# Attention probabilities copied by a DMA into a float32r tile ahead of their transposes, with one raw weight buffer less and one 4 KB buffer more

## The chip, the core and the metric

The kernel runs on one core of a Trainium2 chip. Its time is the device time of one execution in microseconds (us). Three runs of the kernel before took 1148.66 to 1150.13 us, with a median of 1149.91 us. The core has five engines that run beside one another, each through its own list of instructions in a fixed order: TensorE (PE; its weight loads are listed as PEld), VectorE (DVE), ScalarE (ACT), GpSimd (POOL) and SyncE (SP). A DMA is issued by an instruction on one of these lists and then runs on 16 DMA engines that all lists share.

## The reference

Two blocks of one kind, and then a third of another kind, work on 256 tokens of width 1024 in float32. The change touches only the attention of the first two blocks:

```python
sc = jnp.einsum('bqkgd,bskd->bkgqs', qi, ki) * scale          # banded, masked
m = jnp.maximum(jnp.max(sc, axis=-1, keepdims=True), sink_f)
p = jnp.exp(sc - m)
denom = jnp.sum(p, axis=-1, keepdims=True) + jnp.exp(sink_f - m)
o = jnp.einsum('bkgqs,bskd->bqkgd', p / denom, vi)
```

There are 16 query heads of 64 columns on 4 key/value heads, so four query heads share one key/value head. Around the attention, a block projects its normed input to queries, keys, values, three convolution inputs and two gates, mixes attention and convolution through the gates and an output matrix, and then runs a gated feed-forward part of width 2816. The third block has another attention, a pooling part, the same feed-forward shape, and gates made from a conditioning vector.

## The kernel before

**Weights.** All weights lie in DRAM in the order of their use, as 211 pieces of 1 MB. `emit_raw` (L253) loads a piece in two halves of 512 KB on SP's queue into tiles with the tag `raw`, of which there are `NRAW` = 7. `emit_half` (L266) splits each half into a high part `H` (a cast to float32r on ACT, L278) and a low part `L` (a subtraction on DVE, L280); 12 halves of each can stand ready (`NSPLIT`). A raw buffer comes free when its subtraction is done. `get` (L284) is called where a piece is used; it emits the loads and the splits some pieces ahead. Pieces of the conditioning matrix are not split; DVE reduces them straight from the raw tile (L524).

**Matmuls.** The projections are sums of three products of such parts (`mmB` L439, `mmA4` L460, `mmD2` L477). All matmuls made through the helper `mm` bear the line L247.

**Attention.** In each of the first two blocks `attention` (L595) starts eight generators `unit(g, t)`, one for each key/value head g (0 to 3) and each half t of the tokens. A unit goes through these steps:

- L634 and L635: the queries of four heads are split into a high and a low part; L640: four transposes of float32r tiles against `ident_r`; L643: a copy out of PSUM.
- L650 and L651: eight matmuls give the scores S of four heads; L654 to L662: mask, row maximum and bias on DVE.
- L666: four exponentials on ACT write the tile P (128 x 4 x 256, float32, 4 KB in each partition) and its row sums; L668 to L671: denominators; L673: four ACT instructions scale P by the reciprocals.
- L681: eight transposes of 128 x 128 float32 blocks of P against the float32 identity `ident`, in two PSUM tiles of four (the first pair of heads, then the second); L683: ACT copies each PSUM tile into PT.
- For t = 1 the unit goes on to the products of PT with the values (L692).

So there are 16 units and 128 transposes at L681 in all. P and PT are tiles with the tag `s4` (4 KB in each partition, `NS4` = 17 buffers), which also holds activations and gain rows.

**What sets the order.** The kernel's own clock counts time in matmuls: `pe(ns)` (L222) is called behind each group of matmuls with a planned duration, and `tick()` (L225), which is called at a few points inside each projection, resumes the generators that are due. A generator says by `yield d` that it wants to go on d us of this clock later. Between L673 and L681 stands `yield SM_DELAY`, 8.0. The units start `UNIT` = 10 us of this clock apart, beside the convolution projections (`pcc`, `pcx`, `pcb`, `pcp` in the trace). The framework's planner then makes each engine's list from this order, by priorities and its own reckoning of how long each instruction takes: an instruction whose inputs it reckons not to be there yet is passed by others that are. At run time each list is worked through in its order, and an instruction whose input is late holds up all that stand behind it on its engine.

Of the kernel before, what the change touches and what calls it, by code (L numbers as in the profile page):

```python
# [10 lines left out]
F32 = mybir.dt.float32  # L11
F32R = mybir.dt.float32r
# [6 lines left out]
P = 128  # L19
D = 1024  # L20
T = 256
# [12 lines left out]

WARM = 13
WARM2 = 4
NRAW = 7
NSPLIT = 12
LOOK = 3
LOOK_RAW = 5  # L40
NS4 = 17
NS2 = 7
PRIO = 30
TR_DELAY = (6.0, 7.5)
# [2 lines left out]
MIX_DELAY = 2.5  # L47
WO2_LEAD = 2
UNIT = 10.0
SM_DELAY = 8.0  # L50
SOFT = 30
ST_DELAY = 8.0
ST_STEP = 3.5
# [109 lines left out]
def tile_model(ctx: ExitStack, tc: tile.TileContext, x_in, wpack, sink, convw, gains, c_in,  # L163
               b_cond, w_pool, pool_scale, ident_c, rope_c, amask_c, smask_c, tri_c, pmat_c, out):
    nc = tc.nc
# [7 lines left out]
    def s4(name, shape=(P, D), dt=F32):  # L173
        return ac.tile(list(shape), dt, tag="s4", name=name, bufs=NS4)

    def s2(name, shape=(P, 512), dt=F32):
        return ac.tile(list(shape), dt, tag="s2", name=name, bufs=NS2)

    def ps1(name, shape=(P, 512), dt=F32):
        return pp.tile(list(shape), dt, tag="B", name=name, bufs=8)  # L180

    def small(name, n, dt=F32):
        return sm.tile([P, n], dt, tag="sm", name=name, bufs=24)
# [35 lines left out]
    def spawn(gen, delay=0.0):  # L219
        tasks.append([clock[0] + delay, gen])  # L220

    def pe(ns):  # L222
        clock[0] += ns / 1000.0
# [22 lines left out]
    def mm(o, a, b, start, stop, **kw):  # L246
        nc.tensor.matmul(o, a, b, start=start, stop=stop, **kw)  # L247
# [5 lines left out]
    def emit_raw():  # L253
        i, hf = divmod(state["raw"], 2)
        t = wp.tile([P, CH // 2], F32, tag="raw", name=f"raw{i}_{hf}", bufs=NRAW)
        if state["raw"] == 1:
# [55 lines left out]
    ident = cst.tile([P, P], F32, tag="ident", name="ident")  # L312
# [20 lines left out]
    ident_r = cst.tile([P, P], F32R, tag="identr", name="ident_r")  # L333
# [261 lines left out]
    def attention(l, q, kf, v, op):  # L595
        kTh = s4(f"kTh{l}", (P, NKV, T), F32R)
        kTl = s4(f"kTl{l}", (P, NKV, T), F32R)

        def rotate(src, n, t, tg):
            q3 = src.rearrange("p (h d) -> p h d", d=HD)  # L600
            ra = s2(f"r{tg}{l}{t}", (P, 2, n, 16))
            ct = rope[:, t, 0:16].unsqueeze(1).to_broadcast([P, n, 16])
            s0 = rope[:, t, 16:24].unsqueeze(1).to_broadcast([P, n, 8])
            s1 = rope[:, t, 24:32].unsqueeze(1).to_broadcast([P, n, 8])
            nc.vector.tensor_mul(ra[:, 0], q3[:, :, 0:16], ct)
            nc.vector.tensor_mul(ra[:, 1, :, 0:8], q3[:, :, 8:16], s0)
            nc.vector.tensor_mul(ra[:, 1, :, 8:16], q3[:, :, 0:8], s1)
            nc.vector.tensor_add(q3[:, :, 0:16], ra[:, 0], ra[:, 1])

        def keys(t):  # L610
            rotate(kf[t], NKV, t, "k")
            kd = [s2(f"kd{j}{l}{t}", (P, NKV, 2, HD), F32R) for j in range(2)]
            k3 = kf[t].rearrange("p (g d) -> p g d", d=HD)
            for u in range(2):
                nc.scalar.copy(kd[0][:, :, u, :], k3)
            for u in range(2):
                nc.vector.tensor_sub(kd[1][:, :, u, :], k3, kd[0][:, :, u, :].bitcast(F32))
            yield 3.0
            for j, dst in enumerate((kTh, kTl)):
                pk = ps1(f"pk{j}{l}{t}", (P, 4, P), F32R)  # L620
                kdf = kd[j].rearrange("p g u d -> p (g u d)")
                for g in range(NKV):
                    nc.tensor.transpose(pk[:, g, :], kdf[:, g * P:(g + 1) * P], ident_r)
                    pe(64)
                nc.scalar.copy(dst[:, :, t * P:(t + 1) * P], pk.bitcast(F32))
            rotate(q[t], NH, t, "q")
            yield None

        PT = {}

        def unit(g, t):
            qs = s2(f"qs{l}{g}{t}", (P, 4, 2, HD), F32R)
            q3 = q[t].rearrange("p (h d) -> p h d", d=HD)[:, 4 * g:4 * g + 4, :]
            nc.scalar.copy(qs[:, :, 0, :], q3)  # L634
            nc.vector.tensor_sub(qs[:, :, 1, :], q3, qs[:, :, 0, :].bitcast(F32))  # L635
            yield 2.5
            pq = ps1(f"pq{l}{g}{t}", (P, 4, P), F32R)
            qf = qs.rearrange("p h u d -> p (h u d)")
            for hh in range(4):
                nc.tensor.transpose(pq[:, hh, :], qf[:, hh * P:(hh + 1) * P], ident_r)  # L640
                pe(64)
            qT = s2(f"qT{l}{g}{t}", (P, 4, P), F32R)
            nc.scalar.copy(qT, pq.bitcast(F32))  # L643
            yield 2.5
            S = [ps1(f"S{l}{g}{t}{i}", (P, 2, T)) for i in range(2)]
            hs = slice(P, 2 * P) if t == 0 else slice(0, P)
            m = small(f"m{l}{g}{t}", 4)
            for i in range(2):
                for e in range(2):
                    mm(S[i][:, e, :], qT[:, 2 * i + e, :], kTh[:, g, :], True, False)  # L650
                    mm(S[i][:, e, :], qT[:, 2 * i + e, :], kTl[:, g, :], False, True)  # L651
                    pe(214)
                with tc.high_priority(offset=SOFT):
                    nc.vector.tensor_add(S[i][:, :, hs], S[i][:, :, hs],  # L654
                                         amask[:, t, :].unsqueeze(1).to_broadcast([P, 2, P]))
                    nc.vector.reduce_max(m[:, 2 * i:2 * i + 2], S[i], axis=AX.X)
            ns = negsink[:, l, 4 * g:4 * g + 4]
            with tc.high_priority(offset=SOFT):
                nm = small(f"nm{l}{g}{t}", 4)
                nc.vector.scalar_tensor_tensor(nm, m, -1.0, ns, ALU.mult, ALU.min)  # L660
                es = small(f"es{l}{g}{t}", 4)
                nc.vector.tensor_sub(es, nm, ns)  # L662
                den = small(f"den{l}{g}{t}", 4)
                Pt = s4(f"P{l}{g}{t}", (P, 4, T))
                for hh in range(4):
                    nc.scalar.activation(Pt[:, hh, :], S[hh // 2][:, hh % 2, :], AF.Exp, bias=nm[:, hh:hh + 1],  # L666
                                         accum_out=den[:, hh:hh + 1])
                nc.scalar.activation(es, es, AF.Exp)  # L668
                nc.vector.tensor_add(den, den, es)
                rd = small(f"rd{l}{g}{t}", 4)  # L670
                nc.vector.reciprocal(rd, den)  # L671
                for hh in range(4):
                    nc.scalar.activation(Pt[:, hh, :], Pt[:, hh, :], AF.Copy, scale=rd[:, hh:hh + 1])  # L673
            yield SM_DELAY
            if t == 0:
                PT[g] = [s4(f"PT{l}{g}{pr}", (P, 2, 2, T)) for pr in range(2)]
            for pr in range(2):
                pt = ps1(f"PTp{l}{g}{t}{pr}", (P, 2, 2, P))
                for st in range(2):
                    for e in range(2):  # L680
                        nc.tensor.transpose(pt[:, st, e, :], Pt[:, 2 * pr + e, st * P:(st + 1) * P], ident)  # L681
                        pe(107)
                nc.scalar.copy(PT[g][pr][:, :, :, t * P:(t + 1) * P], pt)  # L683
            if t == 0:
                yield None
                return
            yield 2.5
            po = ps1(f"po{l}{g}", (P, 2, T))
            for pr in range(2):
                for st in range(2):  # L690
                    for e in range(2):
                        mm(po[e * HD:(e + 1) * HD, pr, :], v[st][:, g * HD:(g + 1) * HD],  # L692
                           PT[g][pr][:, st, e, :], st == 0, st == 1)
                    pe(482)
            op.put(2 * g, 2, po)
            yield None

        for t in range(2):
            spawn(keys(t), 1.0 + 2.0 * t)
        for i, (g, t) in enumerate((g, t) for g in range(NKV) for t in range(2)):  # L700
            spawn(unit(g, t), 7.0 + UNIT * i)
# [514 lines left out]
```

## Time and profile before

| What | Value |
|---|---|
| Median of three runs | 1149.91 us |
| Profiled execution, its own time | 1148.9 us |
| Its span, from the first to the last instruction | 1146.9 us |
| Busy: PE / PEld / DVE / ACT | 99% / 83% / 70% / 60% |
| DMA, mean over the span | 205 GB/s |
| Attention units, span times of the transposes of P | 71 to 150 us and 497 to 578 us |

The span is shorter than the execution by 2.0 us, which lie before its first and after its last instruction. A row of a group gives the line, the engine, the operation, the tile written and the tiles read, the count, and then the busy time in us and the mean of one instruction in ns; behind it stands how long the engine was idle ahead of these instructions and what ended that. A row of a timeline gives the start in us, the time that the merged instructions took together in us, the engine, the line, the tiles and the count. Matmuls overlap: one matmul's listed duration is its way through the array, and the next starts before it ends, so pace is read from one start to the next.

### The profile page before, as it was taken

Reading aid. Unit: us, or ns where it says so; the run is one execution under the profiler, and the core shown is the slowest. Engines: PE = TensorE matmul, PEld = TensorE weight load, DVE = VectorE, ACT = ScalarE, POOL = GpSimd, SP = SyncE. Lnnn points to the kernel's source line nnn. Section 1 sums busy time; section 2 is a strip of 40 time slices with the busy share of each in tenths; the row PEclk is TensorE's granted clock in tenths of the full one; section 3 lists DMA queues with packets and bytes.
Section 4 is the critical chain, followed back from the end, with each engine's and each line's share of the span. In section 5 each row is a group of like instructions: output and inputs, shape, how many; then the busy total and the mean of one; then the engine's idle time right before and its main releaser. Section 6 shows DMA issues by size and latency. Waiting matters only on the chain. (4 is left out here: it accounts for less than half of the span.)

```text
span 1146.9 us, 15965 instructions
## 1 busy us (share of the span) xinstructions
PE 1135.7 (99%) x5901; PEld 951.2 (83%) x5901; DVE 799.9 (70%) x1190; ACT 686.9 (60%) x1211; POOL 13.4 (1%) x28
## 2 busy tenths in 40 slices
PE   9999999999999999999999999999999999999997
PEld 5888888888888888888888888888888777888886
DVE  7888845858977647798864758867656747865652
ACT  6777866547654446688856557545455847645441
POOL 0000000000000000000000000000000000000000
PEclk9999999999999999999999999999999999999999
DMA  8934346737987752844565538987773653855610
GB/s 299 354 129 149 127 148 203 262 140 250 355 280 238 252 203 91 295 132 153 191 220 204 184 110 287 353 260 242 256 261 108 222 166 103 307 192 183 200 62 37
DMA packets 67039, 235.39 MB, mean 205 GB/s; under 512 B 8849, under 2 KB 9361, under 8 KB 66962
## 3 DMA queue, kind: packets, MB, share of 16 engines
q1 hardware_dynamic: 63216, 224.83, 57.4%
q10 hardware_dynamic: 3746, 9.56, 2.5%
q8 instruction: 46, 0.75, 0.3%
q14 instruction: 31, 0.25, 0.1%
HBM read 233.28 MB, written 1.07 MB: 204 GB/s over the span
## 5 line engine op out<-in xcount | busy, mean ns | idle before, releaser
L280 DVE TENSOR_TENSOR L<-raw,H 128x1024 fp32r<-128x1024 f32 x370 | 444.5, 1220 | 146.8 <-ACT H L278 139.4
L278 ACT CAST H<-raw 128x1024 fp32r<-128x1024 f32 x370 | 382.9, 1052 | 140.7 <-issue 39.1
L247 PE MATMUL dn<-H,fHL 128*128 128x512 f32 x432 | 116.1, 390 | 0.0
L247 PE MATMUL pu<-xf,H 128*128 128x512 f32 x432 | 108.2, 392 | 0.0
L247 PE MATMUL pg<-xf,H 128*128 128x512 f32 x432 | 107.8, 391 | 0.0
L247 PEld LDWEIGHTS dn<-H,fHL 128*128 128x128 f32 x432 | 79.8, 188 | 15.6
L247 PEld LDWEIGHTS pg<-xf,H 128*128 128x128 f32 x432 | 79.2, 188 | 15.2
L247 PEld LDWEIGHTS pu<-xf,H 128*128 128x128 f32 x432 | 77.7, 189 | 13.9
L524 DVE SCALAR_TENSOR_TENSOR raw<-raw,silu_c 128x1024 f32<-128x1024 f32 x48 | 58.2, 1218 | 29.3 <-DMA raw<-in_wpack_dram 29.3
L247 PE MATMUL dn<-L,fHL 128*128 128x512 f32 x216 | 66.6, 389 | 0.0
L247 PEld LDWEIGHTS pg<-xf,L 128*128 128x128 f32 x432 | 58.9, 190 | 4.2
L247 PEld LDWEIGHTS pu<-xf,L 128*128 128x128 f32 x432 | 58.9, 190 | 4.2
L247 PE MATMUL pu<-xf,L 128*128 128x256 f32 x432 | 60.2, 282 | 0.0
L247 PE MATMUL pg<-xf,L 128*128 128x256 f32 x432 | 60.2, 282 | 0.0
L247 PE MATMUL wo<-H,m 128*128 128x512 f32 x192 | 52.5, 395 | 0.0
L571 ACT CAST fHL<-f 128x512 fp32r<-128x512 f32 x27 | 16.8, 621 | 57.4 <-DVE f L569 57.4
L247 PEld LDWEIGHTS dn<-L,fHL 128*128 128x128 f32 x216 | 40.5, 188 | 8.6
L565 ACT ACTIVATE s<-s 128x512 f32<-128x512 f32 x27 | 17.1, 632 | 46.6 <-DVE s L458 46.5
L247 PEld LDWEIGHTS wo<-H,m 128*128 128x128 f32 x192 | 35.4, 188 | 7.6 <-issue 0.6
L247 PE MATMUL pcp<-H,y 128*128 128x512 f32 x128 | 35.2, 395 | 0.0
L247 PE MATMUL pap<-H,o 128*128 128x512 f32 x128 | 35.1, 394 | 0.0
L666 ACT ACTIVATE P<-S,nm 128x256 f32<-128x256 f32 x64 | 29.6, 480 | 8.9 <-DVE nm L660 6.4
(290 smaller groups left out, 1934.5 us busy)
## 6 DMA issues: line engine op xcount, KB each, us to landing
raw<-in_wpack_dram SPq DMA_DIRECT2D x422, 512.0 KB, 5.2
gpm<-in_gains_dram ACTq DMA_DIRECT2D x3, 512.0 KB, 6.8
gpf<-in_gains_dram ACTq DMA_DIRECT2D x3, 512.0 KB, 8.7
gqf<-in_gains_dram ACTq DMA_DIRECT2D x2, 512.0 KB, 6.6
out_dram<-x SPq DMA_DIRECT2D x4, 256.0 KB, 2.0
pmat<-in_pmat_dram SPq DMA_DIRECT2D x2, 384.0 KB, 6.9
x<-in_x_dram SPq DMA_DIRECT2D x2, 256.0 KB, 3.1
x<-in_x_dram SPq DMA_DIRECT2D x1, 512.0 KB, 6.8
```

What stands on the lines that cost most here:

```text
L247: nc.tensor.matmul(o, a, b, start=start, stop=stop, **kw)
L278: nc.scalar.copy(H, r)
L280: nc.vector.tensor_sub(L, r, H.bitcast(F32))
L524: nc.vector.scalar_tensor_tensor(w[u], w[u], 1.0, silu_c, ALU.mult, ALU.mult, accum_out=mcol[:, r, 2 * j + u:2 * j + u + 1])
L565: last = nc.scalar.activation(s, s, AF.Silu)
L571: nc.scalar.copy(fHL[:, 0], fv)
L666: nc.scalar.activation(Pt[:, hh, :], S[hh // 2][:, hh % 2, :], AF.Exp, bias=nm[:, hh:hh + 1], accum_out=den[:, hh:hh + 1])
```

## The change

The scaled probabilities P no longer go straight into the transposes. A DMA issued on ACT's queue copies the whole tile P (512 KB in all) into a second `s4` tile `Pr` of type float32r, and the transposes read `Pr` against `ident_r` and write PSUM tiles of type float32r. The copy out of PSUM reads those as float32. The generator's pause between the scaling and the transposes is 10.5 us of the kernel's clock in place of 8.0, and the clock counts 70 ns for each of these transposes in place of 107. There are 6 raw buffers in place of 7, and 18 `s4` buffers in place of 17; both kinds of buffer take 4 KB in each partition.

```diff
-NRAW = 7
+NRAW = 6
...
-NS4 = 17
+NS4 = 18
...
-SM_DELAY = 8.0
+SM_DELAY = 10.5
...
+            Pr = s4(f"Pr{l}{g}{t}", (P, 4, T), F32R)
+            nc.scalar.dma_start(Pr.bitcast(F32), Pt)
             yield SM_DELAY
             if t == 0:
                 PT[g] = [s4(f"PT{l}{g}{pr}", (P, 2, 2, T)) for pr in range(2)]
             for pr in range(2):
-                pt = ps1(f"PTp{l}{g}{t}{pr}", (P, 2, 2, P))
+                pt = ps1(f"PTp{l}{g}{t}{pr}", (P, 2, 2, P), F32R)
                 for st in range(2):
                     for e in range(2):
-                        nc.tensor.transpose(pt[:, st, e, :], Pt[:, 2 * pr + e, st * P:(st + 1) * P], ident)
-                        pe(107)
-                nc.scalar.copy(PT[g][pr][:, :, :, t * P:(t + 1) * P], pt)
+                        nc.tensor.transpose(pt[:, st, e, :], Pr[:, 2 * pr + e, st * P:(st + 1) * P], ident_r)
+                        pe(70)
+                nc.scalar.copy(PT[g][pr][:, :, :, t * P:(t + 1) * P], pt.bitcast(F32))
```

## The prediction

> **What bounds the kernel now.** I read the page's engine shares first, then the waits of PE, then the line of the transposes, then the timeline of single attention units.
>
> ```profile
> span 1146.9 us, 15965 instructions
> PE 1135.7 (99%) x5901; PEld 951.2 (83%) x5901; DVE 799.9 (70%) x1190; ACT 686.9 (60%) x1211; POOL 13.4 (1%) x28
> PEclk9999999999999999999999999999999999999999
> ```
>
> ```profile
> PE pq L640 <- DVE qs L635: 0.8, 1, 0.8
> PE pq L247 <- DVE Lq L713: 0.8, 1, 0.8
> PE puA L247 <- DVE L L280: 0.6, 1, 0.6
> PE PTp L681 <- ACT P L673: 0.2, 1, 0.2
> ```
>
> PE is busy 99% of the span at a full clock in every slice, and its longest waits are below 1 us each. The end is therefore set by how many instructions PE works through and at what pace. Whatever shortens a PE instruction in the two attention stretches shortens the kernel, and whatever makes PE wait there lengthens it by the whole wait.
>
> ```profile
> L681 PEld LDWEIGHTS PTp<-ident,P x128: 137/141/146, 71.2 to 577.3; 128*128 128x128 f32 x128
> L681 PE MATMUL PTp<-ident,P x128: 270/272/329, 71.3 to 577.4; 128*128 128x128 f32 x128
>   ACT P L673: 1.4, 5
> ```
>
> The line that changes has 128 transposes in 16 groups of eight. PE or its weight loads waited there five times for the scaling of P, 1.4 us in all.
>
> **The cheaper transposes.** The same trace has transposes of float32r tiles, at L640. I take the pace from the weight loads of one group of each kind (start, time together, count):
>
> ```profile
> 68.07 0.42 PEld L640 LDWEIGHTS pq<-ident_r,qs 128*128 128x128 f32 x4
> 68.43 0.19 PEld L247 LDWEIGHTS pcc<-x,H 128*128 128x128 f32 x1
> 71.23 0.90 PEld L681 LDWEIGHTS PTp<-ident,P 128*128 128x128 f32 x8
> 72.10 0.19 PEld L247 LDWEIGHTS S<-kTh,qT 128*128 128x128 f32 x1
> ```
>
> Four float32r transposes take 68.43 - 68.07 = 0.36 us until the next load begins, 0.090 us each. Eight float32 ones take 72.10 - 71.23 = 0.87 us, 0.109 us each. Eight of the new kind would take 8 x 0.090 = 0.72 us, 0.15 us less, and 16 groups 2.4 us less. The bounds come from PE's own rows:
>
> ```profile
> 68.17 0.46 PE L640 MATMUL pq<-ident_r,qs 128*128 128x128 f32 x4
> 68.47 2.08 PE L247 MATMUL pcc<-x,H 128*128 128x512 f32 x8
> 62.58 2.00 PE L247 MATMUL pcb<-x,H 128*128 128x512 f32 x8
> 64.42 1.12 PE L247 MATMUL pcb<-x,L 128*128 128x256 f32 x8
> 65.38 2.00 PE L247 MATMUL pcc<-x,H 128*128 128x512 f32 x8
> ```
>
> From start to start the four take 0.30 us (0.075 each), but the eight matmuls behind them take 2.08 us where eight ordinary ones take 2.00. At 0.075 the gain is 128 x 0.034 = 4.3 us, the upper bound. The delay of the next matmul says that the loads, not the products, set the pace, so I stay with 0.090 and 2.4 us. The lower bound is no gain, if the loads of Pr come no faster than those of P; a loss has no row for it, since both kinds' loads last about 0.14 us.
>
> [...]
>
> **The new wait, and the later start.** The transposes now wait for a DMA of 512 KB that can only be issued when the fourth scaling (L673) is done. How long was P ready ahead of its transposes? ACT's rows and PE's rows of four of the 16 units, the first and the last among them:
>
> ```profile
> 69.42 1.75 ACT L673 ACTIVATE P<-P,rd 128x256 f32<-128x256 f32 x4
> 71.34 1.03 PE L681 MATMUL PTp<-ident,P 128*128 128x128 f32 x8
> 79.72 1.71 ACT L673 ACTIVATE P<-P,rd 128x256 f32<-128x256 f32 x4
> 83.79 1.03 PE L681 MATMUL PTp<-ident,P 128*128 128x128 f32 x8
> 114.61 1.71 ACT L673 ACTIVATE P<-P,rd 128x256 f32<-128x256 f32 x4
> 115.18 1.13 PE L681 MATMUL PTp<-ident,P 128*128 128x128 f32 x5
> 116.61 0.49 PE L681 MATMUL PTp<-ident,P 128*128 128x128 f32 x3
> 572.27 1.71 ACT L673 ACTIVATE P<-P,rd 128x256 f32<-128x256 f32 x4
> 576.69 1.03 PE L681 MATMUL PTp<-ident,P 128*128 128x128 f32 x8
> ```
>
> The first unit is scaled at 69.42 + 1.75 = 71.17 and transposed from 71.34: 0.2 us to spare. The second has 2.4 us, the last 2.7. In the third pair the transposes begin 1.1 us before the scaling ends, in two pieces of five and three. Read so, six of the 16 units had 1.8 to 2.7 us to spare, and ten had from -1.1 to 0.5, on average -0.3.
>
> The pause grows by 2.5 us of the kernel's clock. One half of a projection is eight matmuls of 512 columns and eight of 256, which that clock counts as 8 x 0.213 + 8 x 0.107 = 2.56 us; the rows above take 65.38 - 62.58 = 2.80. So the pause grows by 2.5 x 2.80 / 2.56 = 2.7 us. The ten have then 2.4 us for the DMA, the six 4.5 or more. What it needs (KB, median us from issue to landing, in the first and second attention stretch; all raw loads; the output; an issue on ACT's queue):
>
> ```profile
> raw<-in_wpack_dram SPq DMA_DIRECT2D x24, 512.0 KB, 3.8
> raw<-in_wpack_dram SPq DMA_DIRECT2D x32, 512.0 KB, 4.2
> DMA to landing us min/median/max: 3.1/5.2/9.5
> out_dram<-x SPq DMA_DIRECT2D x4, 256.0 KB, 2.0
> L528 ACTq DMA_DIRECT2D modd<-mcol x6: 329/333/339, 292.0 to 813.6; - x6
> ```
>
> No DMA of this trace goes from SBUF to SBUF. The nearest rows are the 512 KB loads at the same times, 3.8 and 4.2 us; the bounds are 2.0 (half the bytes, nothing else on the engines) and 9.5. I take 3.9. The six have enough. The ten are short by 3.9 - 2.4 = 1.5 us, 15 us together, if their transposes stand in PE's list where the clock puts them. That is the upper bound of the wait; the lower is none. Between them decides the planner. The unit at 115.18 shows that it moves transposes whose P it reckons late: three of eight stand behind two matmuls of `pcc`. As it reckons with ACT's work now and errs by 1.4 us over the run, I let it err by as much with the DMA. The old 1.4 us go, since the DMA's issue on ACT takes them over, and 1.4 us come: nothing in the sum. Behind a waiting transpose stand all matmuls of PE, and ACT's copies out of PSUM (L683, L457) wait for them.
>
> **ACT and the DMA engines.**
>
> ```profile
> 36.00:57.00 21.00, 21.00 (x115) 17.94 (x115) 17.56 (x32) 16.38 (x27) 0.00 (x0) 1.00 0.96 365
> 57.00:151.00 94.00, 93.93 (x593) 80.66 (x592) 76.41 (x167) 76.94 (x190) 0.00 (x0) 1.00 0.38 127
> 480.00:583.00 103.00, 101.89 (x638) 86.11 (x637) 86.92 (x186) 82.48 (x197) 0.00 (x0) 1.00 0.49 161
> ```
>
> Columns: stretch, its length, then PE, PEld, DVE, ACT and POOL busy, clock, DMA share, GB/s. Sixteen issues of 0.33 us are 5.3 us on ACT's list; ACT is idle for 94.0 - 76.9 = 17.1 and 103.0 - 82.5 = 20.5 us in the two stretches, which hides them. The bytes, 16 x 0.5 MB, meet DMA engines that are 38% and 49% busy. Without that cover the issues would delay the casts of weights, which are made far ahead. Pr needs one buffer more while its DMA runs, and there is one more; nothing is counted. If none were free, the issue would hold up ACT.
>
> **One raw buffer less.**
>
> ```profile
> L278 ACT CAST H<-raw 128x1024 fp32r<-128x1024 f32 x370 | 382.9, 1052 | 140.7 <-issue 39.1
> L280 DVE TENSOR_TENSOR L<-raw,H 128x1024 fp32r<-128x1024 f32 x370 | 444.5, 1220 | 146.8 <-ACT H L278 139.4
> 1019.22 5.47 PE dn L247 x24
> raw<-in_wpack_dram SPq DMA_DIRECT2D x33, 512.0 KB, 6.2
> ```
>
> A buffer is held for the landing, the cast and the subtraction: 5.2 + 1.05 + 1.22 = 7.5 us. Six of them pass a half each 7.5 / 6 = 1.25 us, and PE uses one each 5.47 / 2 = 2.7 us. It is tight only at the start, where landing takes 6.2 us: 8.5 / 6 = 1.41 us, beside 512 KB at 365 GB/s, 1.44 us. So I count nothing. The upper bound is that the 33 halves of the first 57 us come a sixth slower, 33 x 0.24 = 7.9 us, with PE taking all of it; its waits for weights there are 0.8 us now.
>
> **The sum,** on the profiled execution's own 1148.9 us (1146.9 of span and 2.0 around it): -2.4 for the transposes, 0 for the waits, 0 for the rest: 1146.5 us. The median of the runs is 1.0 us higher, so the same change from there is 1147.5. I forecast 1146.5. About 0.2%, 2.3 us, is what a measurement of this kernel can tell from no change, and the forecast stands barely beyond it.
>
> **The rivals.**
>
> *The DMA is late where the transposes stand* (chance 0.25). The planner puts the transposes of the ten tight units where the clock does, and PE waits for the landing. For it: only 2.4 us are there and the fastest raw load took 3.1. Against it: the split group at 115.18. Price: 15 us in full, 1148.9 - 2.4 - 1.4 + 15 = 1160.1; while PE waits, ACT and DVE catch up and the next unit is scaled earlier, so about half is likelier, 1152.6. It decides from 3.8 us of waits on, 0.4 us in each of the ten; beyond 6.1 us the kernel is slower by more than 0.2%.
>
> *The transposes get no cheaper* (0.18). [...] 1148.9 us.
>
> *The whole gain* (0.10). The pace is 0.075 us and the planner moves every group far enough, so that the old waits go and none come: 1148.9 - 4.3 - 1.4 = 1143.2.
>
> *Starved at the start* (0.05). Six raw buffers hold the first loads back: up to 1146.5 + 7.9 = 1154.4, about half of it likelier, 1150.5.
>
> **How the numbers follow.** The forecast's own case has 0.42, with a range of its own from 1143.5 to 1149. Faster: 0.37 of it and the 0.10 of the whole gain, 0.47. Slower: most of the late DMA and a little of the start, 0.25. The same: the rest, 0.28. The range goes from 1142, below the whole gain, to 1156, between the half and the full price of the late DMA; about 0.1 lies above and 0.03 below.
>
> **What would show it.** Right: groups of eight at L681 that take about 0.72 us from the first load to the next line's; waits of PE for the DMA of Pr of 2 us or less in all; no new wait of PE for H or L; ACT's issues followed by no idle DVE. Wrong: groups that still take 0.87 us; PE rows at L681 or PEld rows that wait for a DMA of Pr, over 4 us in total; landings of Pr well over 4 us; weights that are waited for before 57 us.

## The result

The changed kernel takes 1177.78 us (median of four runs, 1175.02 to 1181.02) where the kernel before takes 1149.62. The ratio is 1.0248, with a 95% interval from 1.0233 to 1.0262. The kernel is 28 us slower; the forecast was 1146.5, about 3 us faster, and its range ended at 1156.

### The profile page after: what moved, and what is told of

The parts are those of the page before. It is cut to its first block, busy times and chain, and to the rows that moved or that the text cites. A ratio compares the mean times of both kernels' runs of the same rounds, so it can differ in the third digit from the quotient of the medians.

```text
span 1178.1 us, 15989 instructions
## 1 busy us (share of the span) xinstructions
PE 1144.4 (97%) x5901; PEld 955.2 (81%) x5901; DVE 802.3 (68%) x1190; ACT 690.2 (59%) x1211; POOL 13.5 (1%) x28
## 5 line engine op out<-in xcount | busy, mean ns | idle before, releaser
L524 DVE SCALAR_TENSOR_TENSOR raw<-raw,silu_c 128x1024 f32<-128x1024 f32 x48 | 58.0, 1218 | 14.3 <-DMA raw<-in_wpack_dram 14.3
L683 PE MATMUL PTp<-ident_r,Pr 128*128 128x128 f32 x128 | 13.4, 248 | 17.3 <-DMA Pr<-P 15.3
```

The source lines that it names most:

```text
L524: nc.vector.scalar_tensor_tensor(w[u], w[u], 1.0, silu_c, ALU.mult, ALU.mult, accum_out=mcol[:, r, 2 * j + u:2 * j + u + 1])
L683: nc.tensor.transpose(pt[:, st, e, :], Pr[:, 2 * pr + e, st * P:(st + 1) * P], ident_r)
```

## The profile after

The page of the changed kernel, engine shares and the rows of the copy (KB each, median us from issue to landing) and of the transposes (busy us, mean ns, idle us ahead of them and what ended it):

```profile
span 1178.1 us, 15989 instructions
PE 1144.4 (97%) x5901; PEld 955.2 (81%) x5901; DVE 802.3 (68%) x1190; ACT 690.2 (59%) x1211; POOL 13.5 (1%) x28
L683 PE MATMUL PTp<-ident_r,Pr 128*128 128x128 f32 x128 | 13.4, 248 | 17.3 <-DMA Pr<-P 15.3
Pr<-P ACTq DMA_DIRECT2D x16, 512.0 KB, 5.4
```

PE, which was never idle for long, now waits 17.3 us ahead of the transposes. Its share fell from 99% to 97%. The waits of PE, longest first (us in total, times, longest):

```profile
PE PTp L683 <- DMA Pr<-P: 15.3, 9, 3.4
PE ptm L927 <- DVE ga L935: 3.1, 1, 3.1
PE S L247 <- ACT qT L643: 2.1, 3, 1.1
PE PTp L683 <- DVE m L656: 2.0, 1, 2.0
```

The first row is the new wait. The second was 0.5 us in the kernel before. The fourth ended 0.1 us behind the landing of that unit's copy, so it belongs to the first. What one long wait looks like shows in ACT's and PE's timelines around the fourth unit:

```profile
106.44 1.73 ACT L673 ACTIVATE P<-P,rd 128x256 f32<-128x256 f32 x4
108.19 0.50 ACTq L675 DMA_DIRECT2D Pr<-P  x1
...
111.65 1.77 PE L247 MATMUL pcb<-x,H 128*128 128x512 f32 x7
115.97 0.84 PE L683 MATMUL PTp<-ident_r,Pr 128*128 128x128 f32 x8 [2.55 <-DMA Pr<-P]
116.66 1.85 PE L247 MATMUL pcb<-x,L 128*128 128x256 f32 x8
118.30 2.93 PE L247 MATMUL pcc<-x,H 128*128 128x512 f32 x8
```

The scaling ends at 108.17 and the copy is issued at once. PE's work ahead of the transposes lasts until 113.42, so the copy had 5.2 us. It took 7.6, and PE stood still. Then a second loss begins: eight matmuls of `pcc` take 2.93 us, where the prediction's rows have 2.00. The stretches with a lowered clock, one in each row, without the last few us, where both kernels have one (start and end, length, PE, PEld, DVE, ACT, POOL busy, granted clock, DMA share, GB/s):

```profile
116.90:120.30 3.40, 3.40 (x13) 3.01 (x13) 1.67 (x4) 2.88 (x12) 0.00 (x0) 0.50 0.46 151
144.20:147.60 3.40, 3.40 (x12) 2.85 (x11) 3.09 (x9) 3.13 (x8) 0.00 (x0) 0.50 0.30 102
171.50:174.90 3.40, 3.40 (x10) 2.61 (x8) 1.23 (x1) 1.43 (x3) 0.00 (x0) 0.50 0.42 142
233.00:239.70 6.70, 5.74 (x16) 4.71 (x17) 4.90 (x7) 3.86 (x6) 0.00 (x0) 0.50 0.95 355
536.80:540.10 3.30, 3.30 (x10) 2.18 (x10) 2.86 (x5) 1.43 (x4) 0.00 (x0) 0.50 0.57 166
```

PE is at half clock for some 20 us of the attention and gate stretches, each time behind a gap of PE or, at 233 us, within one. The page's row of tenths does not show it, since a slice of 29 us still rounds to 9.

Where the 31.2 us between the two spans went, from the two traces (the traced execution of the changed kernel took 1180.2 us): for each matmul the time from the end of the one before it to its own end, less the median of that for the same tile and shape in the kernel before, summed by kind, less the same sum of the kernel before. An excess of over 0.3 us counts as a gap.

| Kind | us |
|---|---|
| Gaps ahead of the transposes of P | +18.3 |
| Matmuls at half clock | +8.5 |
| Gap at the transposes of the gated mix (`ptm`) | +2.7 |
| Gap ahead of the scores S | +2.9 |
| Gaps in the first 25 us | +1.4 |
| Pace of the 128 transposes | -4.0 |
| The rest | +1.4 |

## The experiments

The theory (called late copy in the expectations): the DMA that copies P shares the DMA engines with the raw loads and lands later than PE reaches the transposes; PE waits, and its clock falls behind the longer waits. The rivals: the missing raw buffer, the traffic of the copies itself, the later start of the transposes, the float32r transposes. In the code below, "..." stands for lines left out.

### The buffers of before in the changed kernel

```diff
-NRAW = 6
+NRAW = 7
-NS4 = 18
+NS4 = 17
```

> The changed kernel with the buffers of before: 7 raw and 17 of 4 KB. Theory (late copy: the DMA of Pr shares the DMA engines with raw loads, lands late, PE waits for it, and the clock falls behind the longest waits): the waits stay, 1173 to 1179 us, with PE waiting 12 us or more for Pr; only the first 25 us lose about 1.5 us of PE's waits. Rival (one raw buffer less is what costs): under 1160 us.

It takes 1178.33 us, ratio 1.0251 (1.0226 to 1.0275). The buffers are not what makes the changed kernel slow. The gap at `ptm` shrinks from 3.4 to 0.8 us, but the gaps ahead of the transposes grow from 18.8 (the 18.3 of the table and the 0.4 that the kernel before has) to 22.9 us; why the one takes the other's place is open. The first 25 us are as before again; they are so in the next run too, with six raw buffers, so the 1.4 us of the table are not the buffer's.

### The buffers alone

```diff
-NRAW = 7
+NRAW = 6
-NS4 = 17
+NS4 = 18
```

> The kernel before with the buffers alone changed: 6 raw and 18 of 4 KB, no DMA of P, float32 transposes. Late copy: 1149.5 to 1152 us, the most of it in the first 25 us. Rival (one raw buffer less is what costs): over 1160 us.

It takes 1154.39 us against 1149.19, ratio 1.0042 (1.0028 to 1.0056). Neither side had the size right: the buffers cost 5 us, not 2 and not 10. ACT's timeline of this kernel, two rows of it, then DVE's and PE's:

```profile
209.88 1.05 ACT L278 CAST H<-raw 128x1024 fp32r<-128x1024 f32 x1 [4.01 <-DMA raw<-in_wpack_dram]
210.83 1.06 ACT L918 ACTIVATE silu_c<-csb 128x1024 f32<-128x1024 f32 x1
...
217.94 0.69 DVE L932 TENSOR_TENSOR ga<-pap,ga 128x512 f32<-128x512 f32 x1
...
220.51 0.63 PE L925 MATMUL ptm<-ident,ga 128*128 128x128 f32 x4 [3.64 <-DVE ga L933]
```

The same place in the kernel before:

```profile
203.20 1.06 ACT L278 CAST H<-raw 128x1024 fp32r<-128x1024 f32 x1 [0.30 <-PE pga L247]
205.84 1.06 ACT L918 ACTIVATE silu_c<-csb 128x1024 f32<-128x1024 f32 x1 [1.58 <-DMA csb<-in_c_dram]
```

With six buffers the cast of a weight that nobody needs yet waits 4.0 us for its load. Behind it on ACT's list stands `silu_c`, behind that on DVE's the first reductions of conditioning weights (L524) and the product `ga`, and behind that PE's transposes, which wait 3.6 us. PE's own waits for weights are within 0.1 us of those before. PE's gaps at `ptm` grow by 3.1 us, those at the transposes of P by about 1, and 1.5 us are lost at half clock.

### The copies, read by nobody

On top of the run before, the DMA is added and the transposes still read P as float32 at a pause of 8.0:

```diff
+            Pr = s4(f"Pr{l}{g}{t}", (P, 4, T), F32R)
+            nc.scalar.dma_start(Pr.bitcast(F32), Pt)
             yield SM_DELAY
```

> The kernel before with the changed buffers and with the 16 DMAs of P into Pr, which nothing reads: the transposes take P as float32 and the pause is 8.0. Late copy: as the run with the buffers alone, within 2 us, since nobody waits for the landing. Rival (the traffic itself: 8 MB more on the DMA engines and 16 issues on ACT's list hold up the weights): 1160 us or more.

It takes 1155.62 us, 1.2 us more than the buffers alone. So the traffic and the 16 issues on ACT's list cost about 1 us; it is the waiting that costs.

### A pause of 16.0, with six raw buffers and with seven

```diff
-SM_DELAY = 10.5
+SM_DELAY = 16.0
```

> The changed kernel with a pause of 16.0 in place of 10.5. Late copy: the longest landing, 7.6 us, is covered, PE waits under 3 us in all for Pr, the clock stays full, 1146 to 1150 us. Rival (the traffic or the buffer): 1165 us or more. Rival (the later start upsets the order of the rest): PE waits move to other lines, 1155 us or more.

With six raw buffers it takes 1153.89 us, ratio 1.0040 (1.0025 to 1.0055), 24 us less than the changed kernel. PE waits 0.9 us for Pr in all, and the clock is full until the end. The time is above what the theory gave, so the same was run with 7 raw and 17 of 4 KB:

> The changed kernel with 7 raw and 17 of 4 KB, and a pause of 16.0. Late copy, with the raw buffer's price apart: the run with 6 raw and 16.0 less 3 to 5 us, 1147 to 1151 us. Rival (what was lost at 16.0 is the later start, not the raw buffer): 1153 us or more.

This takes 1149.11 us, ratio 0.9998 (0.9989 to 1.0007), 4.8 us less: the price of the buffers, measured a second time (the 4 KB buffer more was not tried apart from the raw buffer less). PE waits nowhere for Pr. The traced execution took 1146.95 us, 2.2 us under the median; in it the cheaper transposes give 4.8 us, and gaps elsewhere take more than half of that back, 1.4 us of them waits for S.

### A pause of 13.0, with seven raw buffers

> The changed kernel with 7 raw and 17 of 4 KB, and a pause of 13.0. Late copy: every transpose stands about 2.7 us later than with 10.5, so of the waits for Pr some 3 to 6 us are left in all, and few of them are long enough for the clock to fall: 1150 to 1157 us. Rival (a wait that shifts along with the start): 1170 us or more.

It takes 1160.92 us, ratio 1.0103 (1.0089 to 1.0117), which neither side expected. Wait and landings (least, median, longest):

```profile
  PE PTp L683: 11.6, 7
DMA to landing us min/median/max: 3.0/5.9/7.5
```

From 10.5 to 13.0 the gaps ahead of the transposes fall only from 22.9 to 12.7 us, and one of those left is 4.9 us long. In the changed kernel PE's work ahead of the transposes ended on average 4.9 us behind the scaling and nowhere less than 3.9 (16 units, read as the pair above). The forecast had 2.4 for ten units and at least 4.5 for six, about 3.4 on average by its own readings. With seven raw buffers the average is 4.5 us at 10.5 and 5.8 at 13.0, so a pause of 2.5 us more moved it by 1.3. At 10.5 without the DMA (the run of the later start alone, below) it is 4.0 with a least distance of 1.6. So the planner seems to have moved the units that stood closest to where it reckoned the landing, and a longer pause first uses up that distance. That is inferred from the positions; no run shows the planner's own reckoning.

### The copy on SP's queue

```diff
-            nc.scalar.dma_start(Pr.bitcast(F32), Pt)
+            nc.sync.dma_start(Pr.bitcast(F32), Pt)
```

> The changed kernel with 7 raw and 17 of 4 KB and the pause of 10.5, with the DMA of P issued on SP's queue among the raw loads. Late copy by shared DMA engines: no earlier landing, 1176 us or more, since the issue also stands behind raw loads that wait for a free buffer. Rival (ACT's queue is served worse than SP's): landings of 4 us and under, under 1165 us.

With seven raw buffers and the pause of 10.5 it takes 1160.78 us (two runs), ratio 1.0099 (1.0081 to 1.0118), 17.5 us less than with the copy on ACT's queue. The theory had this wrong. Landings of the copies of P on ACT's queue (first row, from the run with the buffers of before) and on SP's:

```profile
DMA to landing us min/median/max: 3.1/5.4/7.0
```

```profile
DMA to landing us min/median/max: 3.5/4.7/5.6
```

The rival had half of it: the queue matters, but not because every copy is quick on SP's. The longest landings are cut. The idle time of PE ahead of the transposes falls from 20.8 to 12.0 us, no gap there is longer than 2.0, and of six stretches of half clock one is left. Two copies of the changed kernel, on ACT's queue, show what lengthens a landing: the third unit's, with no raw load issued from 92 to 98 us, and the fourth's, beside five raw loads issued from 104.5 to 115.8 us:

```profile
DMA to landing us min/median/max: 2.9/2.9/2.9
DMA to landing us min/median/max: 7.6/7.6/7.6
```

The DMA queues (packets, MB, share of the 16 engines) show where the fourth copy's time went. Its 144 packets are on q10 and the raw loads on q1; the first row is from 108 to 112 us, the other two from 112 to 116, and q10 has no row from 108 to 112:

```profile
q1 hardware_dynamic: 303, 1.13, 95.8%
q1 hardware_dynamic: 201, 0.69, 42.9%
q10 hardware_dynamic: 144, 0.52, 32.1%
```

The copy was issued at 108.19, and its first packet moved 3.9 us later, where the third unit's did so after 1.1 us. In those 3.9 us only raw loads moved on these two queues. From its first packet to its last it took 3.3 us, where the third unit's took 1.4. So in effect this copy first stood behind raw loads, though on a queue of its own, and then shared the engines. Why it came behind them is open. On SP's list the loads that follow are issued after the copy, which fits the shorter tail (5.6 us at most, 7.0 on ACT's queue). That is argued, not shown: there the copy and the loads are on one queue and can't be told apart, and the copy on SP's list also holds the next raw loads back until P is scaled.

### SP's queue and a pause of 13.0; one DMA or two

> The changed kernel with 7 raw and 17 of 4 KB, the DMA of P on SP's queue and a pause of 13.0. Late copy: landings on SP's queue were 5.6 us at most, and the pause adds 2.7 us to the 4 us that were there, so hardly a wait for Pr is left and the cheaper transposes show: 1145.5 to 1149 us. Rival (the wait shifts along with the start): 1155 us or more.

It takes 1146.54 us, ratio 0.9975 (0.9965 to 0.9984): 3.0 us faster than the kernel before, and so faster than both kernels. Its waits of PE, longest first, and then its landings:

```profile
PE warm_ps L247 <- DVE warm L309: 1.5, 1, 1.5
PE S L247 <- ACT qT L643: 0.9, 2, 0.7
```

```profile
DMA to landing us min/median/max: 2.9/5.1/6.2
```

No wait for Pr of over 0.1 us is left. Two DMAs of 256 KB, each behind the two scalings of its heads, came next:

```diff
...
-            nc.scalar.dma_start(Pr.bitcast(F32), Pt)
+                    if hh % 2:
+                        nc.sync.dma_start(Pr.bitcast(F32)[:, hh - 1:hh + 1], Pt[:, hh - 1:hh + 1])
```

> As the run with SP's queue and 13.0, with two DMAs of 256 KB a unit, each issued when the two scalings of its heads are done. Late copy: the first half lands earlier and the second no later, within 1 us of the run with one DMA, 1145.5 to 1149 us. Rival (each further DMA on SP's list holds the raw loads up): 1151 us or more.

This takes 1146.60 us, ratio 0.9976 (0.9966 to 0.9986), no different.

### The later start alone

```diff
-SM_DELAY = 8.0
+SM_DELAY = 10.5
```

> The kernel before with the pause of 10.5 in place of 8.0 and nothing else: no DMA, float32 transposes, 7 raw and 17 of 4 KB. Late copy: the later start by itself costs nothing, 1147.5 to 1150.5 us. Rival (the later start upsets the order of the rest): 1153 us or more.

It takes 1151.13 us, ratio 1.0015 (1.0006 to 1.0024), just above what the theory allowed, with runs from 1149.32 to 1153.12. By the medians it is 1.6 us slower than the kernel before. The traced execution is one of the two slowest, at 1153.1 us. It has a wait of 2.3 us at the transposes of the queries, half clock for 3.4 us behind that, and 1.8 us more of gaps in the first 25 us, ahead of all attention units:

```profile
PE pq L640 <- DVE qs L635: 2.3, 1, 2.3
```

How much of the 1.6 us is the later start's own is therefore open; it is far from 28 us.

### Float32r transposes without any DMA

The scalings write Pr themselves, as float32r, in the kernel before:

```diff
-                    nc.scalar.activation(Pt[:, hh, :], Pt[:, hh, :], AF.Copy, scale=rd[:, hh:hh + 1])
+                    nc.scalar.activation(Pr[:, hh, :], Pt[:, hh, :], AF.Copy, scale=rd[:, hh:hh + 1])
...
```

> The kernel before (7 raw, 17 of 4 KB, pause 8.0) with float32r transposes and no DMA: the four scalings on ACT write Pr as float32r themselves, so P is rounded to float32r, which the changed kernel does not do. Late copy: only the cheaper pace of the transposes is left, 3 to 4 us, 1145 to 1146.5 us. Rival (the float32r transposes are what upsets PE): 1149 us or more.

It takes 1149.14 us, ratio 0.9996 (0.9987 to 1.0004): no gain, against the theory and as the rival had it. The transposes are 3.3 us cheaper in its trace, and small gaps, at those transposes themselves and elsewhere, take all of it back. With the pause of 10.5 and 70 ns for each of these transposes on the kernel's clock:

> The kernel before with the scalings writing Pr as float32r (P is rounded, which the changed kernel does not do), no DMA, 7 raw and 17 of 4 KB, 70 ns of the kernel's clock for each of these transposes and a pause of 10.5. Late copy: with P ready well ahead the small waits that took the gain back at 8.0 go, 1145 to 1147.5 us. Rival (the float32r transposes give nothing that lasts): 1149 us or more.

This takes 1147.20 us, ratio 0.9982 (0.9973 to 0.9991). The distance from the scaling to the end of PE's work ahead of the transposes grew from 0.8 to 3.4 us on average, and no wait for Pr is left. So the gain needs that distance, DMA or not; the pause and the 70 ns were not tried apart.

## Why the prediction was wrong

**The cheaper transposes: right, and a little small.** The forecast took 2.4 us, with 4.3 as its bound. PE's rows of a group of the changed kernel that did not wait:

```profile
99.60 1.09 PE L247 MATMUL pcx<-x,H 128*128 128x512 f32 x4
100.53 0.80 PE L683 MATMUL PTp<-ident_r,Pr 128*128 128x128 f32 x8
101.17 1.18 PE L247 MATMUL pcx<-x,H 128*128 128x512 f32 x4
```

Eight take 0.64 us from start to start, 0.080 us each, and the four matmuls behind them take 1.18 us where the four ahead of them took 1.09. That is 0.73 us in all, as the 0.72 of the forecast. Over the whole kernel the fastest version shows 3.0 us.

**The landing of the copy: the step that failed.** The prediction took 3.9 us for the copy from the raw loads in the same stretches. Those loads run on one queue (q1); the copy came in beside them on a second (q10). It took 5.4 us at the median and up to 7.6, part of it behind raw loads before its first packet moved. A single resource was priced by how it serves its one user, not by how it serves two. This size alone decides: the planner left at least 3.9 us in every unit, so a landing of 3.9 would hardly have been waited for anywhere. As it was, ten of the 16 units waited, nine of them for copies that took 5.4 to 7.6 us.

**"I let it err by as much with the DMA": the second step that failed.** The planner's placing of work on ACT, good to 1.4 us over a run, said nothing about its placing of a DMA. It gave the copies 4.9 us on average, 1.5 more than the forecast had counted, and they were still late in ten units: gaps of 18.3 us, over the upper bound of 15. That this lies near the bound is luck. Of the ten units that the forecast called tight only five waited, and of the six that it gave enough time five did.

**The clock: not in the sum at all.** The late DMA was a named rival, with 1152.6 and 1160.1 us. It ended at 1177.8, since a gap of PE can cost more than its own length: half clock behind the gaps took 8.5 us. Gaps at other places took 7.0 more (the rows of `ptm`, S and the first 25 us). The half that the rival took off, since ACT and DVE would catch up, did not come off. The rival's mechanism was right, its price was not.

**One raw buffer less: counted at nothing, 5 us alone.** The working asked whether weights reach PE in time, and they do. It did not ask what else stands behind a waiting cast on ACT's list. The upper bound of 7.9 us held, but for the start of the kernel and not for the place where it fell due. In the changed kernel this part could not be told from the rest.

**ACT's list and the DMA engines: right.** An issue took about 0.5 us (the row at 108.19), not 0.33, and the copies that nobody reads cost 1.2 us in all.

## What to carry to other kernels

A copy through a DMA in a chain that a full engine waits for is priced by its worst landing beside the other transfers (7.6 us in the changed kernel), not by a median (5.4), and the queue it is issued on is a choice worth a run: here it was 17.5 us at the same pause. Take the distance between producer and consumer first, then the cheaper instruction: the same transposes gave nothing, 3 us gained, or 28 us lost, mainly by how far ahead their input was. A buffer pool is checked against everything that stands behind its waiting instructions on their engines, not only against the transfers it feeds.

## What the runs showed of the hardware

PE's clock was halved for 3.4 us at a time, once for 6.8, at gaps of PE between 1.7 and 3.1 us (the transposes at 170.03 us came 1.7 us behind the last matmul, and the clock fell at 171.5). Not every such gap did it: one of 3.4 us ahead of 589.55 us left the clock full. So in this trace the length of a gap does not tell whether the clock falls.

The five stretches begin at 116.89, 144.19, 171.50, 232.94 and 536.73 us. The first three rows are the 3.4 us ahead of the first three of them; the last two rows are two stretches of 3.4 us that each hold a part of the gap ahead of 589.55 (start and end, length, then PE busy, PEld and the rest as above):

```profile
113.47:116.89 3.42, 0.92 (x10) 0.95 (x11) 2.29 (x7) 1.40 (x2) 0.00 (x0) 1.00 0.51 194
140.78:144.19 3.41, 1.25 (x13) 1.25 (x13) 3.41 (x9) 3.34 (x12) 0.00 (x0) 1.00 0.36 113
168.09:171.50 3.41, 1.68 (x13) 1.38 (x13) 1.23 (x1) 1.76 (x3) 0.00 (x0) 1.00 0.44 149
584.51:587.93 3.42, 1.65 (x12) 1.33 (x10) 3.42 (x10) 2.68 (x9) 0.00 (x0) 1.00 0.82 296
587.93:591.34 3.41, 1.79 (x13) 1.65 (x14) 2.10 (x5) 1.79 (x7) 0.00 (x0) 1.00 0.61 202
```

PE was idle for 2.50, 2.16 and 1.73 us in the first three and for 1.77 and 1.62 us in the last two. What decides whether the clock falls was not shown, so which gap costs the clock as well could not be told ahead of a run.
